# A decoder block's planned part: weight pages held through a seven-product pass, whole-tile additions on VectorE, longer transfer times in the planner

## The chip, the core and the metric

The kernel runs on one core of one Trainium2 chip. TensorE (PE) multiplies matrices into eight PSUM banks, VectorE (DVE), ScalarE (ACT) and GpSimd (POOL) do elementwise work, and SyncE (SP) issues most transfers between memory and the on-chip SBUF. The metric is the device time of one execution in microseconds; the median over several runs counts.

## The reference

One decoder layer for 1024 tokens of width 1024, all in float32:

```
h    = RMSNorm(x)
P    = h @ w_in                        # 1024 x 3584, split among the head groups
ret  = retention(rotary(rq), rotary(rk) / 8, rv)      # 8 heads of 64, chunks of 128, decaying state
ret  = RMSNorm per head(ret) * silu(rg)
dif  = (softmax(q1 k1) - lam * softmax(q2 k2)) v      # 4 heads, causal, RMS norm on q and k, per-head norm
x    = x + concat([ret, dif]) @ w_out
x    = x + (silu(h2 @ w_gate) * (h2 @ w_up)) @ w_down  # h2 = RMSNorm(x), inner width 2816
```

The columns rq, rk, rv, rg of `w_in` (512 each) belong to the retention heads; the change touches how their projection, the retention itself and the first feed-forward block are prepared.

## The kernel before

Each float32 product is made of three matmuls (`mm3`): a matrix is split into a high part `hi` (a cast, on ScalarE) and a low part `lo = a - hi` (a subtraction, on VectorE), and hi·hi, hi·lo and lo·hi are added up in a bank. So every weight tile of 128x512 needs a load, a cast and a subtraction before TensorE can use it (`halves_`).

The program has three parts. First the differential heads run, software-pipelined with their projection, to about 270 us. Last, from about 650 us, ten more blocks of the feed-forward part and the down projection run. Between them lies the **planned part**, which the change touches. It has no fixed loop order: each piece of work is a job with an engine, an estimated duration (`dur`, and `lag` for the time after a transfer's issue) and the pages it reads and writes. `Plan.times` runs a list scheduling over these estimates, in four rounds; each main job of TensorE gets a goal, and every other job a latest time counted back from the main jobs it serves (`AHEAD` us before) or from its `due`. The jobs are then issued in the order of planned times, and each engine keeps that order strictly: an instruction that waits holds up all behind it on its engine, and a transfer whose page is not free holds up all later ones on SP.

The planned part holds, in this order of TensorE's main work:

- Two **passes** (p = 0, 1, four heads each) over the retention projection, as a seven-product scheme for 2x2 blocks. Pass 0 has P4, P6, P7, P5, P3 left to do (P1 and P2 lie ahead), pass 1 has P1, P2, P6, P5, P3, P7, P4. Each product is 4 token tiles (j) of 4 contraction tiles (k), 12 matmuls per token tile. Its left operand is a block of `hT`, or a sum of blocks that was written to memory earlier and comes back through two pages (`x_sum`, transfers `raw<-sumd`). Its weights are blocks of `w_in` or signed sums of them, made in `prepare(p, name, k, n)`: load 256 KB blocks into pages (`rawload`, from the ring `wraw` of 13 pages named `spare`, `rowa`, `pr` in the profile), add, scale with the norm gain, split. Every product loads its own blocks anew. With a, b, d, c for the blocks (0,0), (0,1), (1,0), (1,1) of one k: P1 uses a, P2 d, P3 c, P5 a − b, P6 a − b + c, P7 b − c, P4 (d − c) − (a − b), up to the gains.
- Sixteen **retention units** (`unit(p, t)`): load a token tile's projections (`rowa<-cd`), rotary, transposes, two small score matmuls, decay mask, state update, output, per-head norm and gate. TensorE's parts of a unit (`m<-cs,wx` 128x128, `h<-wx,wy`, `h<-wy`, `h<-wy,wx`) stand between main matmuls.
- The **output projection** (`o_proj`, 16 products of 24 matmuls) with transposes of its input (`mix_turn`), then the second norm, transposes (`norm`) and block sums for the feed-forward part (`f_sum`).
- The **first feed-forward block**: seven products for w_gate and seven for w_up (`first_weights`, `first_product`), of whose weight sums five each add two tiles.

In the profile nearly all instructions have line 136, the helper that issues them; tile names tell them apart. `whi`/`wlo` are weight splits, `sx`, `act`, `sb`, `b`, `wo` hold operand blocks, `sum` and `raw` the sums, `wx` and `wy` the pages of the units, `h`, `pp`, `m` are banks.

Of the kernel before, what the change touches and what calls it, by code (L numbers as in the profile page):

```python
# [107 lines left out]
def block_kernel(ctx: ExitStack, tc: tile.TileContext, x, norm1_g, w_in, ret_norm_g, dq_g, dk_g,  # L108
# [685 lines left out]
    GAP, GAP_PE, AHEAD = 0.15, 0.6, 4.0  # L794
# [4 lines left out]
    def dma(to, src, r=(), w=(), **kw):  # L799
        return add("SP", 0.06, lambda: SY.dma_start(to, src), r, w, lag=2.6, **kw)  # L800
# [6 lines left out]
    def tt(to, a, b, op, r, w, eng="DVE", dur=0.78, **kw):  # L807
        e = V if eng == "DVE" else G
        return add(eng, dur, lambda: e.tensor_tensor(out=to, in0=a, in1=b, op=op), r, w, **kw)

    def stt(to, a, scalar, b, op0, op1, r, w, dur=0.78, **kw):
        return add("DVE", dur, lambda: V.scalar_tensor_tensor(out=to, in0=a, scalar=scalar, in1=b, op0=op0, op1=op1),
                   r, w, **kw)
# [24 lines left out]
    wraw = Ring([spare[i] for i in (0, 4, 5, 7, 1)] + rowk[4:8] + held)  # L838
# [7 lines left out]

    def rawload(p, kap, nu, k):
        key, page = wraw()
        dma(page.rearrange("p (a b) -> p a b", b=256), win_block(p, nu, 4 * kap + k), (), [key])
# [10 lines left out]
    def difference(p, k):  # L860
        (ka, a), (kb, b) = rawload(p, 0, 0, k), rawload(p, 0, 1, k)
        tt(a, a, b, ALU.subtract, [ka, kb], [ka], "POOL", 1.45)
        return (ka, a), (kb, b)

    def prepare(p, name, k, n):
        ga, gb = g1(k), g1(4 + k)
        if name in ("P1", "P2", "P3"):
            key, page = rawload(p, *{"P1": (0, 0), "P2": (1, 0), "P3": (1, 1)}[name], k)
            halves_(n, key, page, gb if name != "P1" else ga)
        elif name == "P5":  # L870
            (ka, a), _ = difference(p, k)
            halves_(n, ka, a, ga)
        elif name == "P6":
            (ka, a), (kb, b) = difference(p, k)
            kc, c = rawload(p, 1, 1, k)
            act_copy(b, a, [ka], [kb], ga)
            stt(c, c, gb, b, ALU.mult, ALU.add, [kb, kc], [kc])
            halves_(n, kc, c)
        elif name == "P7":
            (kb, b), (kc, c) = rawload(p, 0, 1, k), rawload(p, 1, 1, k)  # L880
            act_copy(c, c, [kc], [kc], gb)
            stt(b, b, ga, c, ALU.mult, ALU.subtract, [kb, kc], [kb])
# [3 lines left out]
        else:  # L886
            (ka, a), (kb, b) = difference(p, k)
            (kd, d), (kc, c) = rawload(p, 1, 0, k), rawload(p, 1, 1, k)
            tt(d, d, c, ALU.subtract, [kd, kc], [kd], "POOL", 1.45)
            act_copy(b, a, [ka], [kb], ga)  # L890
            stt(d, d, gb, b, ALU.mult, ALU.subtract, [kb, kd], [kd])
# [40 lines left out]
    for name in ("P4", "P6", "P7", "P5", "P3"):  # L932
# [4 lines left out]
        for j in range(4):  # L937
# [8 lines left out]
            elif name == "P7":  # L946
                tt(v, u, m, ALU.subtract, [bk, uk], [vk], dur=0.7)
                tt(d, d, v, ALU.subtract, [dk, vk], [dk], "POOL", 1.45)
# [64 lines left out]
    def unit(p, t, due=None):  # L1013
# [4 lines left out]
        for rk, r_, at in ((rck, rc, C_COS), (rnk, rn, C_SIN)):  # L1018
            tb = cs[:, at + t * 32:at + (t + 1) * 32].unsqueeze(1).broadcast_to([P, 16, 32])
            tt(r_.rearrange("p (g d) -> p g d", d=32), ca.rearrange("p (g d) -> p g d", d=32), tb, ALU.mult,  # L1020
               [cak], [rk], "DVE" if at == C_COS else "POOL", 0.78 if at == C_COS else 1.45)
# [3 lines left out]
        tt(q4[:, :, 0, :], rc4[:, :, 0, :], rn4[:, :, 1, :], ALU.subtract, [rck, rnk], [qk], "POOL", 0.8)  # L1025
        tt(q4[:, :, 1, :], rc4[:, :, 1, :], rn4[:, :, 0, :], ALU.add, [rck, rnk, qk], [qk], "POOL", 0.8)
        vk, vh = vh_r()
        tt(vh.rearrange("p (g d) -> p g d", d=HD), cb[:, 0:256].rearrange("p (g d) -> p g d", d=HD),
           vdec[:, t, 4 * p:4 * p + 4].unsqueeze(2).broadcast_to([P, 4, HD]), ALU.mult, [cbk], [vk], dur=0.46,
           )  # L1030
# [43 lines left out]
        def out_():  # L1074
# [15 lines left out]
        tt(onr[1].rearrange("p (g d) -> p g d", d=HD), o4, rs_.unsqueeze(2).broadcast_to([P, 4, HD]), ALU.mult,  # L1090
           ["b7o", sk], [onr[0]], dur=0.45)
        if p == 0 and t < 4:
            tt(gs, onr[1], gs, ALU.mult, [onr[0], gk_], [gk_], "POOL", 0.8)
# [462 lines left out]
```

## Time and profile before

| | |
|---|---|
| Median of 3 runs | 1241.63 us (1240.04 to 1241.9) |
| The profiled execution | 1242.88 us, of which the profile's span is 1240.8 us |
| TensorE, VectorE, ScalarE, GpSimd busy | 1196.0, 907.5, 570.6, 666.3 us |
| Mean granted TensorE clock | 0.99 |
| Planned part (from P4 to the end of the first feed-forward block) | 278.8 to 649.3 us |

A row of the groups gives engine, operation, output <- inputs, shape and count, then busy time and mean duration in ns of one, then the engine's idle time before them and what ended it. A row of the windows gives the stretch, its length, the busy time of each engine with its instruction count, the granted TensorE clock (1.00 is full speed), the busy share of the DMA engines and GB/s. A row of the transfers gives the queue, the count, the size and the median us from issue to landing. A row of a timeline gives start, duration, engine, operation, and in brackets the idle time before it and what ended it.

### The profile page before, as it was taken

The numbers are of one execution on the slowest core, as the hardware profiler recorded it, in microseconds if no ns is written. First come the engines' busy times: TensorE is split into PE (matmuls) and PEld (weight loads), VectorE is DVE, ScalarE is ACT, GpSimd is POOL, SyncE is SP. The second block draws the span as 40 slices with busy tenths as digits, with TensorE's granted clock in tenths as the row PEclk, the third lists the DMA queues.
The fourth block names the chain that finished last, engine by engine and source line by source line (L and its number), as shares of the span: only waits on it lengthen the run. The fifth ranks groups of instructions, "written<-read, shape, count | busy, mean of one in ns | idle before, by whom it ended". The sixth has DMA issues, their size and how long they took to land.

```text
span 1240.8 us, 17596 instructions
## 1 busy us (share of the span) xinstructions
PE 1196.0 (96%) x5872; PEld 1009.0 (81%) x5872; DVE 907.5 (73%) x1460; ACT 570.6 (46%) x1188; POOL 666.3 (54%) x728
## 2 busy tenths in 40 slices
PE   8999999999898999999979999999999999999998
PEld 7898989877677778887858888888888888888887
DVE  6988888866857975546898666666676659698697
ACT  6766555644434443334544434334334344444442
POOL 2678777562336746532576665455655447154053
PEclk9999999999999999999989999999999999999999
DMA  7166677269877753321223332233332268943332
GB/s 201 64 145 101 94 141 133 79 209 319 280 240 257 254 187 123 110 85 52 77 68 111 112 127 101 89 103 108 111 125 79 81 205 296 365 147 101 96 109 87
DMA packets 132953, 178.97 MB, mean 144 GB/s; under 512 B 12800, under 2 KB 77440, under 8 KB 132736
## 3 DMA queue, kind: packets, MB, share of 16 engines
q1 hardware_dynamic: 125920, 167.30, 41.5%
q0 software_dynamic: 5760, 10.49, 6.5%
q8 instruction: 46, 0.75, 0.3%
q14 instruction: 43, 0.35, 0.1%
q10 hardware_dynamic: 1184, 0.07, 0.1%
HBM read 125.65 MB, written 54.26 MB: 145 GB/s over the span
## 4 chain that ended last, share of the span: by engine, by line
PE 78%; DMA 6%; DVE 6%; POOL 4%; issue 3%; ACT 2%; SPq 0%; DVEq 0%; POOLq 0%; ACTq 0%
PE h L136 34%; PE pp L136 25%; PE m L136 17%; PE big L136 2%; DMA spare<-in_w_in_dram 2%; DVE wlo L136 1%; DMA raw<-sumd 1%; DMA rowa<-in_w_in_dram 1%; POOL sum L136 1%; POOL spare L136 1%; DVE pr L136 1%; POOL wx L136 0%; DMA sumd<-sumd 0%; ACT whi L136 0%; DVE sx L136 0%
## 5 line engine op out<-in xcount | busy, mean ns | idle before, releaser
L136 POOL TENSOR_TENSOR sum<-rawp 128x512 f32<-128x512 f32 x100 | 142.5, 1427 | 146.0 <-DVE wlo L136 141.3
L136 PE MATMUL pp<-whi,act 128*128 128x384 f32 (+1 forms) x624 | 191.7, 358 | 1.2 <-ACT whi L136 0.7
L136 ACT CAST whi<-sum 128x512 fp32r<-128x512 f32 x155 | 96.3, 622 | 198.6 <-PE h L136 65.1
L136 DVE TENSOR_TENSOR wlo<-sum,whi 128x512 fp32r<-128x512 f32 x155 | 154.2, 995 | 35.3 <-ACT whi L136 35.2
L136 POOL TENSOR_TENSOR sum<-wide 128x512 f32<-128x512 f32 x55 | 85.8, 1560 | 128.5 <-DVE wlo L136 98.9
L136 PEld LDWEIGHTS pp<-whi,act 128*128 128x128 f32 x624 | 116.2, 189 | 6.2 <-ACT whi L136 0.9
L136 PE MATMUL h<-sx,whi 128*128 128x512 f32 x360 | 112.6, 394 | 7.4 <-ACT rowa L136 7.1
L136 PE MATMUL pp<-wlo,act 128*128 128x384 f32 (+1 forms) x312 | 108.6, 348 | 0.6 <-DVE wlo L136 0.6
L136 DVE TENSOR_TENSOR wlo<-wide,whi 128x512 fp32r<-128x512 f32 x99 | 79.2, 824 | 32.9 <-ACT whi L136 32.8
L136 ACT CAST whi<-wide 128x512 fp32r<-128x512 f32 x99 | 59.4, 621 | 85.2 <-PE m L136 43.2
L136 PEld LDWEIGHTS h<-sx,whi 128*128 128x128 f32 x360 | 67.4, 189 | 21.6 <-ACT rowa L136 7.6
L136 POOL TENSOR_TENSOR fsum<-c 128x512 f32<-128x512 f32 x50 | 71.9, 1450 | 10.1 <-DMA ffd<-fsum 10.1
L136 PE MATMUL h<-whi 128*128 128x512 f32 x196 | 76.5, 390 | 0.0
L136 DVE TENSOR_TENSOR wlo<-rawp,whi 128x512 fp32r<-128x512 f32 x44 | 46.4, 1055 | 41.1 <-ACT whi L136 40.3
L136 DVE TENSOR_TENSOR c<-c,h 128x512 f32<-128x512 f32 x80 | 53.0, 683 | 32.1 <-PE h L136 32.0
L136 PE MATMUL h<-whi,wlo 128*128 128x512 f32 x196 | 76.3, 389 | 0.0
L136 PE MATMUL h<-wlo,whi 128*128 128x512 f32 x196 | 76.2, 389 | 0.0
L136 PE MATMUL h<-sx,wlo 128*128 128x512 f32 x180 | 70.5, 392 | 0.4 <-DVE wlo L136 0.4
L136 PEld LDWEIGHTS pp<-wlo,act 128*128 128x128 f32 x312 | 59.3, 190 | 3.6 <-DVE wlo L136 1.2
L136 PE MATMUL h<-b,whi 128*128 128x512 f32 x176 | 54.3, 390 | 0.0
L136 ACT ACTIVATE p<-big,nm 128x128 f32<-128x128 f32 (+7 forms) x64 | 47.7, 745 | 6.0 <-DVE nm L136 5.4
L136 DVE TENSOR_REDUCE nm<-big 128x1 f32<-128x128 f32 (+7 forms) x64 | 48.5, 758 | 2.2
(302 smaller groups left out, 3253.0 us busy)
## 6 DMA issues: line engine op xcount, KB each, us to landing
wide<-ffd SPq DMA_DIRECT2D x77, 256.0 KB, 2.8
spare<-in_w_in_dram SPq DMA_DIRECT2D x69, 256.0 KB, 4.7
ffd<-fsum SPq DMA_DIRECT2D x55, 256.0 KB, 2.0
rawp<-in_w_gate_dram SPq DMA_DIRECT2D x22, 512.0 KB, 3.7
rawp<-in_w_up_dram SPq DMA_DIRECT2D x22, 512.0 KB, 3.6
wide<-in_w_down_dram SPq DMA_DIRECT2D x44, 256.0 KB, 5.4
sumd<-act POOLq DMA_DIRECT2D x40, 256.0 KB, 5.6
rowa<-cd SPq DMA_DIRECT2D x32, 256.0 KB, 3.2
```

The costliest lines, as they stand in the source:

```text
L136: i = getattr(self.engine, op)(*(now(a) for a in args), **{k: now(a) for k, a in kw.items()})
```

## The change

- **Held weight pages.** In each pass P6 now loads a and c of each k into eight pages that stay for the pass (`keep_r`, `held_w`): a is overwritten with a − b, c stays. P5 and P3 split from these pages and load nothing, P7 loads only b, and pass 1's P4 only d. `wraw` has five pages left. P7 puts c times its gain into a page of its own.
- **From GpSimd to VectorE:** the weight differences, one subtraction of P7's outputs, in each unit the product with the sine, the two rotary halves and the gate product, the block sums 2, 5 and 6 and the weight sums of w_up.
- **From VectorE to ScalarE:** in each unit the scaling of v and of the output per head, each one operation of 256 columns, becomes four of 64 columns.
- **The planner's numbers:** a transfer occupies SP 0.8 us instead of 0.06, with 2.4 instead of 2.6 us behind it; VectorE operations count 0.74 or 0.75 instead of 0.78 or 0.8; `AHEAD` is 8 instead of 4 us; the units of tiles 4 to 7 are due at the projections of tiles 0 and 1.

```
-    GAP, GAP_PE, AHEAD = 0.15, 0.6, 4.0
+    GAP, GAP_PE, AHEAD = 0.15, 0.6, 8.0
-        return add("SP", 0.06, lambda: SY.dma_start(to, src), r, w, lag=2.6, **kw)
+        return add("SP", 0.8, lambda: SY.dma_start(to, src), r, w, lag=2.4, **kw)
-    def tt(to, a, b, op, r, w, eng="DVE", dur=0.78, **kw):
+    def tt(to, a, b, op, r, w, eng="DVE", dur=0.74, **kw):
-    def stt(to, a, scalar, b, op0, op1, r, w, dur=0.78, **kw):
+    def stt(to, a, scalar, b, op0, op1, r, w, dur=0.74, **kw):
...
-    wraw = Ring([spare[i] for i in (0, 4, 5, 7, 1)] + rowk[4:8] + held)
+    wraw = Ring(rowk[4:8] + [prk[8]])
+    keep_r = Ring([spare[i] for i in (0, 4, 5, 7, 1, 2, 6, 3)])
...
     g1 = lambda c: g1col[:, c:c + 1]
+    def load_raw(key, page, p, kap, nu, k):
+        dma(page.rearrange("p (a b) -> p a b", b=256), win_block(p, nu, 4 * kap + k), (), [key])
+
     def rawload(p, kap, nu, k):
         key, page = wraw()
-        dma(page.rearrange("p (a b) -> p a b", b=256), win_block(p, nu, 4 * kap + k), (), [key])
+        load_raw(key, page, p, kap, nu, k)
         return key, page
     def halves_(n, key, src, scale=None, reads=()):
...
         else:
             stt(lo, src, scale, hi.bitcast(F32), ALU.mult, ALU.subtract, [key, f"wh{n}"], [f"wl{n}"])
-    def difference(p, k):
-        (ka, a), (kb, b) = rawload(p, 0, 0, k), rawload(p, 0, 1, k)
-        tt(a, a, b, ALU.subtract, [ka, kb], [ka], "POOL", 1.45)
-        return (ka, a), (kb, b)
+    held_w = {}
     def prepare(p, name, k, n):
         ga, gb = g1(k), g1(4 + k)
-        if name in ("P1", "P2", "P3"):
-            key, page = rawload(p, *{"P1": (0, 0), "P2": (1, 0), "P3": (1, 1)}[name], k)
-            halves_(n, key, page, gb if name != "P1" else ga)
+        if name in ("P1", "P2"):
+            key, page = rawload(p, *{"P1": (0, 0), "P2": (1, 0)}[name], k)
+            halves_(n, key, page, ga if name == "P1" else gb)
+        elif name == "P6":
+            a, c = keep_r(), keep_r()
+            held_w[k] = a, c
+            (ka, a), (kc, c) = a, c
+            load_raw(ka, a, p, 0, 0, k)
+            kb, b = rawload(p, 0, 1, k)
+            load_raw(kc, c, p, 1, 1, k)
+            tt(a, a, b, ALU.subtract, [ka, kb], [ka])
+            act_copy(b, a, [ka], [kb], ga)
+            stt(b, c, gb, b, ALU.mult, ALU.add, [kb, kc], [kb])
+            halves_(n, kb, b)
         elif name == "P5":
-            (ka, a), _ = difference(p, k)
-            halves_(n, ka, a, ga)
-        elif name == "P6":
-            (ka, a), (kb, b) = difference(p, k)
-            kc, c = rawload(p, 1, 1, k)
-            act_copy(b, a, [ka], [kb], ga)
-            stt(c, c, gb, b, ALU.mult, ALU.add, [kb, kc], [kc])
-            halves_(n, kc, c)
+            halves_(n, *held_w[k][0], ga)
+        elif name == "P3":
+            halves_(n, *held_w[k][1], gb)
         elif name == "P7":
-            (kb, b), (kc, c) = rawload(p, 0, 1, k), rawload(p, 1, 1, k)
-            act_copy(c, c, [kc], [kc], gb)
-            stt(b, b, ga, c, ALU.mult, ALU.subtract, [kb, kc], [kb])
+            kb, b = rawload(p, 0, 1, k)
+            kt, t_ = wraw()
+            kc, c = held_w[k][1]
+            act_copy(t_, c, [kc], [kt], gb)
+            stt(b, b, ga, t_, ALU.mult, ALU.subtract, [kb, kt], [kb])
             halves_(n, kb, b)
         elif p == 0:
             halves_(n, *held[k])
         else:
-            (ka, a), (kb, b) = difference(p, k)
-            (kd, d), (kc, c) = rawload(p, 1, 0, k), rawload(p, 1, 1, k)
-            tt(d, d, c, ALU.subtract, [kd, kc], [kd], "POOL", 1.45)
-            act_copy(b, a, [ka], [kb], ga)
-            stt(d, d, gb, b, ALU.mult, ALU.subtract, [kb, kd], [kd])
+            (ka, a), (kc, c) = held_w[k]
+            kd, d = rawload(p, 1, 0, k)
+            tt(d, d, c, ALU.subtract, [kd, kc], [kd])
+            act_copy(a, a, [ka], [ka], ga)
+            stt(d, d, gb, a, ALU.mult, ALU.subtract, [ka, kd], [kd])
             halves_(n, kd, d)
     BLOCK = {"P1": hT[0][0], "P2": hT[0][1], "P4": hT[1][1], "P5": sxt[0], "P6": sbt, "P7": sxt[1], "P3": sxt[2]}
...
-                tt(d, d, v, ALU.subtract, [dk, vk], [dk], "POOL", 1.45)
+                tt(d, d, v, ALU.subtract, [dk, vk], [dk])
...
-               [cak], [rk], "DVE" if at == C_COS else "POOL", 0.78 if at == C_COS else 1.45)
+               [cak], [rk])
-        tt(q4[:, :, 0, :], rc4[:, :, 0, :], rn4[:, :, 1, :], ALU.subtract, [rck, rnk], [qk], "POOL", 0.8)
-        tt(q4[:, :, 1, :], rc4[:, :, 1, :], rn4[:, :, 0, :], ALU.add, [rck, rnk, qk], [qk], "POOL", 0.8)
+        tt(q4[:, :, 0, :], rc4[:, :, 0, :], rn4[:, :, 1, :], ALU.subtract, [rck, rnk], [qk], dur=0.46)
+        tt(q4[:, :, 1, :], rc4[:, :, 1, :], rn4[:, :, 0, :], ALU.add, [rck, rnk, qk], [qk], dur=0.46)
-        tt(vh.rearrange("p (g d) -> p g d", d=HD), cb[:, 0:256].rearrange("p (g d) -> p g d", d=HD),
-           vdec[:, t, 4 * p:4 * p + 4].unsqueeze(2).broadcast_to([P, 4, HD]), ALU.mult, [cbk], [vk], dur=0.46,
-           )
+
+        def scale_v():
+            for h in range(4):
+                A.activation(vh[:, h * HD:(h + 1) * HD], cb[:, h * HD:(h + 1) * HD], AF.Copy,
+                             scale=vdec[:, t, 4 * p + h:4 * p + h + 1])
+        add("ACT", 0.95, scale_v, [cbk], [vk])
...
-        tt(onr[1].rearrange("p (g d) -> p g d", d=HD), o4, rs_.unsqueeze(2).broadcast_to([P, 4, HD]), ALU.mult,
-           ["b7o", sk], [onr[0]], dur=0.45)
+
+        def scale_o():
+            for h in range(4):
+                A.activation(onr[1][:, h * HD:(h + 1) * HD], bank[7][:, h * HD:(h + 1) * HD], AF.Copy,
+                             scale=rs_[:, h:h + 1])
+        add("ACT", 0.95, scale_o, ["b7o", sk], [onr[0]])
-            tt(gs, onr[1], gs, ALU.mult, [onr[0], gk_], [gk_], "POOL", 0.8)
+            tt(gs, onr[1], gs, ALU.mult, [onr[0], gk_], [gk_], dur=0.46)
-            tt(m_[:, 256 * p:256 * p + 256], onr[1], gs, ALU.mult, [onr[0], gk_], [mk], "POOL", 0.8)
+            tt(m_[:, 256 * p:256 * p + 256], onr[1], gs, ALU.mult, [onr[0], gk_], [mk], dur=0.46, due=due)
...
+    DUE1 = {4: ("o", 0, 1), 5: ("o", 1, 1), 6: ("o", 1, 1), 7: ("o", 1, 1)}
+
-            unit(0, t)
-        unit(1, t)
+            unit(0, t, marks[DUE1[t]])
+        unit(1, t, marks[DUE1[t]] if t >= 4 else None)
...
-        eng, dur, e = ("POOL", 1.45, G) if b in (2, 5, 6) else ("DVE", 0.8, V)
+        eng, dur, e = ("DVE", 0.75, V)
...
-            eng, dur, e = ("POOL", 1.45, G) if o else ("DVE", 0.8, V)
+            eng, dur, e = ("DVE", 0.75, V)
```

Since the planner sets the order, the change moves instructions on all engines. Three places follow.

SP's queue where pass 0 begins: `mixdd<-rowa` spills rows of the differential heads' output (here those of the last two tiles), `in_w_in` are weight blocks, `raw<-sumd` the left operands' sums, `cd<-pr` results. Before:

```order
L136 DMA mixdd<-rowa 128x512
L136 DMA spare<-in_w_in_dram 128x2x256 x5
L136 DMA mixdd<-rowa 128x512
L136 DMA rowa<-in_w_in_dram 128x2x256 x2
L136 DMA spare<-in_w_in_dram 128x2x256
L136 DMA rowa<-in_w_in_dram 128x2x256
L136 DMA raw<-sumd 128x512 x2
```

Now:

```order
L136 DMA mixdd<-rowa 128x512
L136 DMA spare<-in_w_in_dram 128x2x256
L136 DMA mixdd<-rowa 128x512
L136 DMA spare<-in_w_in_dram 128x2x256
L136 DMA rowa<-in_w_in_dram 128x2x256
L136 DMA spare<-in_w_in_dram 128x2x256
L136 DMA rowa<-in_w_in_dram 128x2x256
L136 DMA spare<-in_w_in_dram 128x2x256
L136 DMA rowa<-in_w_in_dram 128x2x256
L136 DMA spare<-in_w_in_dram 128x2x256 x2
```

Four loads of P6 (of the first row's five; the other belongs to P4) moved from ahead of the last spill to behind it.

TensorE between the last matmuls of pass 1's P4 and the output projection: turns (`m<-cs,wx`), scores (`h<-wx,wy`), state (`h<-wy,wx`) and output (`h<-wy`) of units, and turns of the projection's input (`m<-cs,rowa`, `pp<-cs,pr`). Before:

```order
L136 MATMUL m<-cs,wx 128x128 x4
L136 MATMUL h<-wy 128x64 x4
L136 MATMUL h<-wy,wx 128x128 x2
L136 MATMUL m<-cs,rowa 128x128 x4
L136 MATMUL h<-wx,wy 128x256 x2
L136 MATMUL h<-wy,wx 128x128 x2
L136 MATMUL m<-cs,wx 128x128 x4
L136 MATMUL m<-cs,rowa 128x128 x4
```

Now:

```order
L136 MATMUL m<-cs,wx 128x128 x4
L136 MATMUL h<-wy,wx 128x128 x2
L136 MATMUL pp<-cs,pr 128x128 x4
L136 MATMUL m<-cs,rowa 128x128 x4
L136 MATMUL h<-wy,wx 128x128 x2
L136 MATMUL h<-wy 128x128
L136 MATMUL h<-wy 128x64 x2
L136 MATMUL h<-wy 128x128
L136 MATMUL h<-wy 128x64 x2
L136 MATMUL h<-wx,wy 128x256 x2
```

This run of small matmuls has 11 rows where it had 16 (both cut here); the units' remaining parts stand among the first seven products of the projection, where before they reached into the thirteenth.

VectorE at the end of the first feed-forward block: `rowa<-rowa,m` and `pr<-pr,pp` add products into outputs, `rowa<-rowa,pr` multiplies with the gate, `wlo<-sum,whi` and `wlo<-rawp,whi` are splits of the next block's weights. Before:

```order
L136 TENSOR_TENSOR wlo<-sum,whi 128x512
L136 TENSOR_TENSOR pr<-pr,pp 128x512
L136 TENSOR_TENSOR wlo<-sum,whi 128x512
L136 TENSOR_TENSOR rowa<-rowa,pp 128x512 x2
L136 TENSOR_TENSOR rowa<-rowa,m 128x512
L136 TENSOR_TENSOR wlo<-sum,whi 128x512
L136 TENSOR_TENSOR rowa<-rowa,m 128x512
L136 TENSOR_TENSOR rowa<-rowa,pr 128x512 x2
```

Now:

```order
L136 TENSOR_TENSOR rowa<-rowa,pp 128x512 x2
L136 TENSOR_TENSOR rowa<-rowa,h 128x512
L136 TENSOR_TENSOR pr<-pr,h 128x512
L136 TENSOR_TENSOR pr<-pr,pp 128x512
L136 TENSOR_TENSOR rowa<-rowa,m 128x512 x2
L136 TENSOR_TENSOR rowa<-rowa,pr 128x512 x4
L136 TENSOR_TENSOR wlo<-sum,whi 128x512
L136 TENSOR_TENSOR wlo<-rawp,whi 128x512
```

All splits of the next block moved behind the last addition and the four gate products. On TensorE the next block's first product stood among the last planned ones; now the first two matmuls of each of its first four products, eight in all, stand right behind the last planned one and their third waits for a split.

More of the change, by code (lines that the diff above doesn't have):

```diff
@@ L1242, in f_sum @@
         add("ACT", 0.62, lambda: A.copy(hi, opened["sum"][n]), [f"sum{n}"], [f"k{b}{p}h"], after=blk_after[b])
-        add("DVE", 0.8, lambda: V.tensor_tensor(out=lo, in0=opened["sum"][n], in1=hi.bitcast(F32), op=ALU.subtract),
+        add("DVE", 0.75, lambda: V.tensor_tensor(out=lo, in0=opened["sum"][n], in1=hi.bitcast(F32), op=ALU.subtract),
             [f"sum{n}", f"k{b}{p}h"], [f"k{b}{p}l"])
@@ L1291, in first_weights @@
         add("ACT", 0.65, lambda: A.copy(hi, src()), [key], [f"wh{at}"])
-        add("DVE", 0.8, lambda: V.tensor_tensor(out=lo, in0=src(), in1=hi.bitcast(F32), op=ALU.subtract),
+        add("DVE", 0.75, lambda: V.tensor_tensor(out=lo, in0=src(), in1=hi.bitcast(F32), op=ALU.subtract),
             [key, f"wh{at}"], [f"wl{at}"])
```

## The prediction

> **What bounds the kernel now.** I read the busy shares first, then the windows by stage, then what TensorE waited for, and last the chain and the groups where those waits are longest.
>
> ```profile
> PE 1196.0 (96%) x5872; PEld 1009.0 (81%) x5872; DVE 907.5 (73%) x1460; ACT 570.6 (46%) x1188; POOL 666.3 (54%) x728
> core 0: us, PE busy (x) PEld busy (x) DVE busy (x) ACT busy (x) POOL busy (x), PEclk, DMA share, GB/s
> 278.80:300.00 21.20, 18.96 (x72) 14.09 (x71) 12.96 (x18) 10.55 (x19) 6.72 (x5) 0.92 1.04 345
> 300.00:360.00 60.00, 53.46 (x230) 42.27 (x229) 43.10 (x58) 22.58 (x38) 16.87 (x12) 1.00 0.83 272
> 360.00:428.00 68.00, 60.77 (x285) 48.82 (x284) 52.39 (x74) 33.36 (x59) 44.35 (x43) 0.97 0.76 245
> 428.00:600.00 172.00, 166.24 (x894) 141.04 (x894) 108.57 (x184) 67.98 (x150) 77.27 (x108) 0.98 0.37 119
> 600.00:649.30 49.30, 40.53 (x189) 32.88 (x186) 44.52 (x52) 24.89 (x45) 35.40 (x22) 0.93 0.17 53
> 649.30:1200.00 550.70, 550.70 (x2430) 456.00 (x2431) 392.18 (x506) 224.92 (x387) 282.61 (x196) 1.00 0.42 137
> ```
>
> TensorE is the bound, and from 649.3 us on it never idles: 550.70 us for 2430 matmuls, 0.227 us each. The change touches only the planned part, 278.8 to 649.3. There TensorE idles 2.2, 6.5, 7.2, 5.8 and 8.8 us in the five stages, 30.5 together. To this comes a lowered clock: 0.92, 0.97, 0.98 and 0.93 of the stages' lengths leave 1.7, 2.0, 3.4 and 3.5 us, about 10.6. So some 41 us is all there is to win. The stages: the start of pass 0; the rest of pass 0 and the start of pass 1; the end of pass 1 with the retention units; the output projection; the first feed-forward block.
>
> **The loads of the passes.** From 278.8 to 428 the DMA engines are 76% busy or more. The second view has the weight loads of both passes, the third the chain at its longest wait.
>
> ```profile
> DMA packets 38095, 47.09 MB, mean 262 GB/s; under 512 B 2877, under 2 KB 27709, under 8 KB 38082
> spare<-in_w_in_dram SPq DMA_DIRECT2D x54, 256.0 KB, 5.0
> rowa<-in_w_in_dram SPq DMA_DIRECT2D x28, 256.0 KB, 5.0
> pr<-in_w_in_dram SPq DMA_DIRECT2D x6, 256.0 KB, 4.8
> 312.27 4.84 DMA raw<-sumd
> 317.14 0.63 ACT sx L136
> 317.79 0.70 DVE sx L136
> 318.51 2.85 DMA raw<-sumd
> raw<-sumd SPq DMA_DIRECT2D x10, 256.0 KB, 4.7
> raw<-in_x_dram SPq DMA_DIRECT2D x6, 256.0 KB, 2.9
> ```
>
> 54, 28 and 6 make 88 loads, as the code has it: 8 for each of four k in pass 0, 14 in pass 1. The change leaves 4 and 7, that is 44: 11.5 MB of the 47.1 MB of 270 to 450 us go, a quarter.
>
> What waits there is less the weights than the activation sums: sixteen tiles (`raw<-sumd`) pass through two pages. A page's round is load 4.84, split 0.63 and 0.70, 6.2 us together; TensorE eats two tiles in 24 matmuls, 5.45 us. Twelve of the tiles (P7, P5, P3) fall behind 300 us: six rounds, each 0.75 us too slow, make 4.5 of the 6.5 us idle in 300 to 360; I put the rest down to late weights. With a quarter less traffic the DMA share falls from 0.83 to about 0.62. The two landing rows bound the load: 4.7 us as in 300 to 333, 2.9 us as in 520 to 600, where the DMA engines have little else (119 GB/s and less). Between them in proportion to the share I take 4.0; the round is then 5.3 us, just under 5.45. **Gain 5 us**, the 4.5 and a little of the late weights; with 4.7 nothing, with 2.9 all 6.5.
>
> The Trainium skill ("DMA: Bandwidth & Descriptors", Anatomy of one DMA) puts a transfer at about 2.0 us plus its bytes at 436 GB/s, an estimate of 2.6 us for 256 KB. The trace disagrees: its median stays at 2.9 us where the engines are nearly free and at 4.7 us where they are busy. By the rule the gain here would be the whole 6.5 us.
>
> The start of pass 0 may lose. On SP's queue the last spill of the attention rows now stands ahead of all loads of P6; before, four of these were issued ahead of it.
>
> ```profile
> 269.25 5.88 SPq L136 DMA_DIRECT2D spare<-in_w_in_dram  x5
> 275.74 0.34 SPq L136 DMA_DIRECT2D mixdd<-rowa  x1
> ```
>
> Four loads of 0.26 MB at the 345 GB/s of this stage cost 3.0 us if they come last; in return half as many loads compete from 276 us on. The last weights of P6 pass a subtraction, two scalings and a split behind them. **0**, from a loss of 3.0 to a gain of 3.9 (idle and clock).
>
> **GpSimd's tiles on VectorE.** The rows are of 272 to 650 us.
>
> ```profile
> L136 POOL TENSOR_TENSOR sum<-pr 128x512 f32<-128x512 f32 x4 | 6.5, 1642 | 0.0
> L136 DVE TENSOR_TENSOR sx<-sum,sx 128x512 fp32r<-128x512 f32 x8 | 11.4, 1428 | 2.1 <-ACT sx L136 1.8
> L136 DVE TENSOR_TENSOR pr<-pr,h 128x512 f32<-128x512 f32 x26 | 17.6, 678 | 0.1
> L136 DVE TENSOR_TENSOR raw<-rawp 128x512 f32<-128x512 f32 x5 | 3.4, 690 | 0.1
> L136 DVE TENSOR_TENSOR wlo<-sum,whi 128x512 fp32r<-128x512 f32 x5 | 4.2, 849 | 2.5 <-ACT whi L136 2.5
> 599.53 0.68 DVE L136 TENSOR_TENSOR sum<-pr,rowa 128x512 f32<-128x512 f32 x1
> 600.13 0.69 DVE L136 TENSOR_TENSOR raw<-rawp 128x512 f32<-128x512 f32 x1
> 627.41 1.22 PE L136 MATMUL h<-sx,whi 128*128 128x512 f32 x2 [7.15 <-ACT rowa L136]
> 649.28 0.70 PE L136 MATMUL m<-b,whi 128*128 128x512 f32 x2 [0.66 <-DVE rowa L136]
> ```
>
> One addition of two tiles takes GpSimd 1.64 us and VectorE 0.69; back to back VectorE starts one each 0.60 us. And a VectorE operation with both inputs in SBUF takes 1.43 us beside GpSimd's additions, 0.69 where it has none beside it, while one that reads a PSUM bank keeps 0.68. So the two engines' additions run one after the other anyway, and what moves costs less than the wait it ends.
>
> *First feed-forward block.* 17 additions move (twelve block sums, five weight sums). VectorE has 52 operations in 44.5 us now; with 17 more, and the five splits `wlo<-sum` of the next block going later, it has 64: 38 us at 0.60, 44 at 0.68. TensorE has 40.5, less 3.5 of lost clock and less 2.7 for one product of the next block that stands in this stage only before. The stage without that product is 46.6 us now and would be about 41: 5.6 us. The 7.15 us wait should go: its releaser is ScalarE's copy of a bank into a `rowa` page, and GpSimd's late sums still read those pages.
>
> But the seam gets worse. Before, the next block's first splits stand between the last planned operations of VectorE, and the wait there is 0.66 us. Now they stand behind the last addition and four gate products: 0.68, four times 0.60 and 0.68 for the split make 3.8 us, against eight matmuls (1.8 us) that TensorE has ready. That is 2.0 us instead of 0.7. **Gain 4 us** net; bounds 0 (VectorE at 0.68 and the whole 3.8 exposed) and 12.3 (neither idle nor lost clock).
>
> *Retention units*, sixteen of them:
>
> ```profile
> L136 POOL TENSOR_TENSOR wx<-rowa,cs 128x512 f32<-128x512 f32 x16 | 23.5, 1467 | 0.5
> L136 POOL TENSOR_TENSOR wx<-wx 128x256 f32<-128x256 f32 x32 | 27.7, 885 | 14.9 <-PE h L136 10.1 <-DVE wx L136 4.6
> L136 DVE TENSOR_TENSOR wx<-h,small 128x256 f32<-128x256 f32 x16 | 6.7, 420 | 6.3 <-POOL small L136 6.1
> L136 ACT ACTIVATE whi<-spare,g1col 128x512 fp32r<-128x512 f32 x16 | 10.9, 715 | 4.1 <-issue 4.0
> L136 ACT ACTIVATE wy<-rowa,rs 128x256 f32<-128x256 f32 x16 | 8.1, 509 | 22.8 <-DMA mixrd<-wy 15.0 <-POOL pr L136 7.8
> ```
>
> The rotary steps go from 1.47 and twice 0.89 on GpSimd, 3.2 us, to 2.2 on VectorE (two at 0.69, two at 0.42). Each head scaling goes from one VectorE operation of 0.42 to four on ScalarE. No 64-column scaling is in the trace: 0.715 for 512 and 0.509 for 256 columns continue to 0.35, four are 1.4 us one by one; bounds 1.0 if they overlap by a quarter, 2.0 at the 0.509 row. One unit's path is thus shorter by 1.0 and longer by 1.0 per scaling at its end: about even. ScalarE gains 32 times 1.4, 45 us, on 159 us busy in 370: it has room.
>
> What shortens is the wait in 360 to 428: GpSimd, 44 us busy there, makes the weight differences between the rotary steps, and matmuls wait for either. Differences fall from 24 to 12 and leave GpSimd. Of 7.2 us idle and 2.0 us of clock I take **5 us**, from 0 (the units' own chain is what decides) to 9.
>
> In 428 to 600 the units of t=4 to 7 now end by the middle of the projection instead of three quarters through; the second half is left with transposes alone, the first half is denser on VectorE and ScalarE. Of 5.8 and 3.4 us I take **4 us**, from a loss of 4 (the denser half idles as the end of pass 1 does now, at 7.2 of 68 us) to 9.
>
> **The sum:** 5 + 0 + 4 + 5 + 4 = 18 us. The profiled execution took 1242.88 us (span 1240.8 and 2.1 around it), 1.25 above the median of 1241.63: 1242.88 − 18 − 1.25 = 1223.6, so **1224 us**.
>
> **Rivals.** *More goes than I take* (0.14): the planner's transfer and VectorE times now stand near the measured ones (0.8 plus 2.4 us against 2.9 to 4.7; 0.74 against 0.69), so few waits come unplanned; six us of idle and none of the lost clock stay: 1242 − 35 = 1207. Against it: the seam and the dense units are new waits.
>
> *The loads were hidden* (0.11): rounds stay at 6.2 us since bursts, not the mean, set the landing, and the 5 us of pass 0 stay out, as do those of 360 to 428: 1234. For it speaks the SP order, in which the sums still stand between weights.
>
> *No change* (0.06): as that, and the seam and the dense half take back the rest: 1241.
>
> *Slower* (0.11): the clock. The granted clock drops where small matmuls stand close together:
>
> ```profile
> 520.00:528.50 8.50, 7.64 (x35) 7.10 (x34) 5.66 (x10) 3.26 (x7) 6.50 (x9) 0.60 0.34 92
> 627.00:632.00 5.00, 4.59 (x13) 3.63 (x14) 4.75 (x5) 2.72 (x6) 5.00 (x4) 0.63 0.31 97
> ```
>
> At 520 us TensorE was busy 7.64 of 8.5 us and still had 0.60: this is a run of unit matmuls and transposes. Twelve units now stand in the end of pass 1 and the first half of the projection, a stretch about as long as the third stage, 68 us. All of it at 0.60 costs 45 us; from 0.40 of it on the 18 us are gone, and 0.5 of it gives 1242 − 18 + 23 = 1247. Against it: the longest run of small matmuls now is cut by projection matmuls.
>
> The Trainium skill ("TensorE: Matmul & The Clock Gate", What's actually happening) has the clock halve after about 3.4 us idle. By that this rival falls away; the trace disagrees at 520 us, where 0.86 us of 8.5 were idle.
>
> **Chances.** My case 0.58, with its own range 1214 to 1234. A measurement here tells 0.2%, 2.5 us: faster 0.58 + 0.14 + 0.11 = 0.83, same 0.06, slower 0.11. The range of 8 in 10 leaves half of the best case and the slower one outside: 1208 to 1240.
>
> **What would show it.** DMA share 300 to 360 near 0.6 and `raw<-sumd` landing in 4 us; GpSimd below 10 us busy in the first feed-forward block and `sx<-sum,sx` at 0.69; a wait of 2 to 3 us at the seam; the clock at 0.95 or more over the units. I am wrong if the five stages together idle more than 20 us, or if `raw<-sumd` still lands in 4.7.

## The result, and the profile after

The changed kernel takes 1209.3 us (median of 4 runs, 1206.9 to 1210.8), the kernel before 1241.0 on the same chip. The ratio is 0.9743, with a 95% interval of 0.9724 to 0.9762: 31.7 us less. The forecast was 1224, with a range from 1208 to 1240: the direction held, and the gain was 1.8 times the 18 us of the sum.

The page's busy line, and the windows of the changed kernel, cut where it reaches the work at which the five stages of the kernel before began and ended:

```profile
PE 1188.1 (98%) x5872; PEld 1003.9 (83%) x5872; DVE 909.9 (75%) x1525; ACT 601.2 (50%) x1316; POOL 536.7 (44%) x619
core 0: us, PE busy (x) PEld busy (x) DVE busy (x) ACT busy (x) POOL busy (x), PEclk, DMA share, GB/s
278.80:297.00 18.20, 17.85 (x79) 14.49 (x78) 14.17 (x22) 12.22 (x21) 0.00 (x0) 1.00 0.92 303
297.00:350.30 53.30, 52.80 (x223) 40.82 (x223) 44.54 (x70) 28.40 (x46) 1.00 (x2) 1.00 0.77 241
350.30:406.80 56.50, 56.50 (x278) 47.47 (x277) 46.19 (x81) 30.38 (x69) 6.81 (x11) 1.00 0.53 165
406.80:573.50 166.70, 163.30 (x888) 137.51 (x888) 113.39 (x206) 93.65 (x257) 37.47 (x62) 0.99 0.42 130
573.50:614.80 41.30, 38.58 (x191) 32.35 (x189) 40.20 (x67) 24.20 (x45) 3.16 (x3) 1.00 0.19 60
```

The five stages took 21.2, 60.0, 68.0, 172.0 and 49.3 us; they take 18.2, 53.3, 56.5, 166.7 and 41.3. That is 3.0, 6.7, 11.5, 5.3 and 8.0 us; of the last, about 2.7 us come back behind the seam, the border to the next block, so 5.3 are gained. These are four matmuls of the next block (0.9 us; before, twelve of them stood in this stage, now eight) and 1.9 us of a lowered clock that is shown below. Together 31.8 us, the difference of the two spans (1240.8 and 1209.0). The cuts follow the main products; a few of the units' small matmuls have moved across them, so the third and fourth figure may each be off by a us or two.

By cause it reads more simply. TensorE idled 30.5 us between 278.8 us and the seam, and idles 7.0 now. It is busy 329.0 us there instead of 340.0. Of these 10.9 us, 0.9 are the four matmuls; the other 10.0 are lowered clock that is gone, and 1.9 of them come back behind the seam. 23.5 and 10.0 less 1.9 make 31.6. The two largest of what TensorE still waits for from 270 to 650 us (3.0 us in four other rows):

```profile
PE h L136 <- DVE wlo L136: 2.3, 2, 2.0
PE h L136 <- DVE wy L136: 2.2, 2, 1.7
```

The columns are the total, the number of waits and the longest one. The longest is the seam that the prediction named, 1.98 us behind VectorE's four gate products, and the chain there shows how it ends:

```profile
611.01 0.75 DVE rowa L136 x2
...
612.22 1.89 DVE rowa L136 x3
614.11 0.61 DVE wlo L136
...
614.77 4.14 PE h L136 x10
618.91 2.29 PE m L136 x10
```

The ten matmuls behind the wait take 4.14 us, the ten after them 2.29: in this execution the wait costs almost as much again in clock. (The last section has other runs with the same wait where it does not.)

### The profile page after: what moved, and what is told of

It is laid out like the page before. It is cut to its first block, busy times and chain, and to the rows that moved or that the text cites. A ratio compares the mean times of both kernels' runs of the same rounds, so it can differ in the third digit from the quotient of the medians.

```text
span 1209.0 us, 17487 instructions
## 1 busy us (share of the span) xinstructions
PE 1188.1 (98%) x5872; PEld 1003.9 (83%) x5872; DVE 909.9 (75%) x1525; ACT 601.2 (50%) x1316; POOL 536.7 (44%) x619
## 4 chain that ended last, share of the span: by engine, by line
PE 82%; DVE 7%; DMA 5%; ACT 3%; issue 2%; POOL 2%; SPq 0%; ACTq 0%; DVEq 0%; POOLq 0%
PE h L136 37%; PE pp L136 25%; PE m L136 17%; PE big L136 2%; DMA raw<-sumd 2%; DVE wlo L136 1%; DMA spare<-in_w_in_dram 1%; DVE sx L136 1%; DVE sum L136 1%; ACT wx L136 0%; DVE wy L136 0%; DMA sumd<-sumd 0%; DMA more<-in_w_in_dram 0%; POOL spare L136 0%; DMA rowa<-in_w_in_dram 0%
## 5 line engine op out<-in xcount | busy, mean ns | idle before, releaser
L136 DVE TENSOR_TENSOR wlo<-sum,whi 128x512 fp32r<-128x512 f32 x155 | 158.0, 1019 | 34.0 <-ACT whi L136 33.6
```

What stands on the lines that cost most here:

```text
L136: i = getattr(self.engine, op)(*(now(a) for a in args), **{k: now(a) for k, a in kw.items()})
```

## The experiments

Each run was timed in five rounds beside the kernel before. "Above the changed kernel" is the difference of the two ratios to the kernel before, times 1240 us; both intervals together leave such a difference uncertain by about 3 us.

| run | what it is | ratio to before (95%) | us |
|---|---|---|---|
| `a_old_numbers` | after, all old planner numbers | 0.9804 (0.9790 to 0.9817) | 7.6 above after |
| `a_old_dma` | after, old transfer cost only | 0.9793 (0.9780 to 0.9807) | 6.2 above |
| `a_reload` | after, 88 weight loads (and 12 more differences on VectorE) | 0.9820 (0.9806 to 0.9833) | 9.5 above |
| `a_pool_ff` | after, 17 FF additions on GpSimd | 0.9841 (0.9828 to 0.9854) | 12.2 above |
| `a_port` | after, 17 idle additions on GpSimd | 0.9856 (0.9841 to 0.9870) | 14.0 above |
| `a_dve_scale` | after, head scalings on VectorE | 0.9849 (0.9836 to 0.9862) | 13.1 above |
| `a_pool_units` | after, rotary and gating on GpSimd | 0.9750 (0.9737 to 0.9763) | 0.9 above |
| `a_pool_diff` | after, weight differences on GpSimd | 0.9739 (0.9726 to 0.9752) | 0.5 below |
| `a_seam` | after, gate products behind three splits | 0.9722 (0.9708 to 0.9735) | 2.6 below |
| `b_new_numbers` | before, new planner numbers only | 0.9953 (0.9936 to 0.9970) | 5.8 below before |
| `b_held` | before, held weights only | 0.9934 (0.9923 to 0.9946) | 8.2 below before |
| `b_ff` | before, 17 FF additions on VectorE only | 0.9935 (0.9920 to 0.9949) | 8.1 below before |

### The loads of the passes: `a_reload` and `b_held`

`a_reload` puts before's rings and weight preparation back, with the differences on VectorE:

```
-    wraw = Ring(rowk[4:8] + [prk[8]])
-    keep_r = Ring([spare[i] for i in (0, 4, 5, 7, 1, 2, 6, 3)])
+    wraw = Ring([spare[i] for i in (0, 4, 5, 7, 1)] + rowk[4:8] + held)
...
+        elif name == "P5":
+            (ka, a), _ = difference(p, k)
```

where `difference` loads both of its weights again, as in the kernel before. So the run has not only 44 loads more: VectorE also makes 24 differences instead of 12 (1537 operations in all instead of 1525, 918.0 us busy instead of 909.9).

> The changed kernel with all 88 weight loads back (before's rings and weight preparation, differences on VectorE). Theory W: the 10 us that the stages from 278.8 to 336 us gained were the loads' doing; 1217 to 1220 us, raw<-sumd landing in 4.5 us or more. Rival (the traffic was hidden, the order did it): within 3 us of the changed kernel, 1209 to 1212 us.

It is 9.5 us above the changed kernel, but not where either theory had it. Windows of this run:

```profile
300.00:340.00 40.00, 39.11 (x170) 31.12 (x169) 36.13 (x58) 17.78 (x29) 0.00 (x0) 1.00 1.00 330
435.00:500.00 65.00, 56.80 (x325) 47.50 (x326) 50.98 (x99) 42.92 (x131) 19.90 (x28) 0.97 0.41 126
```

and of the changed kernel:

```profile
300.00:340.00 40.00, 39.50 (x164) 29.86 (x163) 33.85 (x54) 18.47 (x29) 0.00 (x0) 1.00 0.88 281
435.00:500.00 65.00, 62.67 (x360) 53.51 (x361) 50.55 (x99) 45.92 (x139) 21.59 (x33) 0.97 0.49 148
```

With the DMA engines busy all of 300 to 340 us, TensorE idles there 0.9 us instead of 0.5. The time goes later, 435 to 500 us: 8.2 us idle instead of 2.3, in a stretch of retention units. Which transfer, page or VectorE operation makes the late units later was not isolated. One candidate is their data (`rowa<-cd`, 340 to 440 us), in the changed kernel first and then in `a_reload`:

```profile
rowa<-cd SPq DMA_DIRECT2D x17, 256.0 KB, 2.8
```

```profile
rowa<-cd SPq DMA_DIRECT2D x19, 256.0 KB, 4.2
```

Against it: of the fifteen units whose first transposes the trace has, the first eleven start within 2.2 us of each other in the two runs; only the last four are 5.6 to 8.1 us late.

`b_held` does the opposite to the kernel before: the held pages alone, and the twelve differences that are left on GpSimd.

> The kernel before with held weights alone: 44 loads less, 12 of the 24 weight differences less, the rest still on GpSimd. By the prediction's first and third terms 5 to 10 us below before, ratio 0.992 to 0.996, with raw<-sumd landing in 4 us. Rival (transfers were not what the passes waited for): 0 to 3 us below, ratio 0.998 or more, and what goes comes from GpSimd's missing differences.

8.2 us below before, as the prediction's terms would have it; whether it is the loads or the twelve differences less on GpSimd, this run does not part; the activation sums land in 3.6 us here (300 to 333 us). The wait of the first feed-forward block stays (5.8 us, on the same `rowa` copy). So alone the held pages are worth about what undoing them costs.

### The planner's numbers: `a_old_numbers`, `a_old_dma` and `b_new_numbers`

```
-    GAP, GAP_PE, AHEAD = 0.15, 0.6, 8.0
+    GAP, GAP_PE, AHEAD = 0.15, 0.6, 4.0
-        return add("SP", 0.8, lambda: SY.dma_start(to, src), r, w, lag=2.4, **kw)
+        return add("SP", 0.06, lambda: SY.dma_start(to, src), r, w, lag=2.6, **kw)
-    def tt(to, a, b, op, r, w, eng="DVE", dur=0.74, **kw):
+    def tt(to, a, b, op, r, w, eng="DVE", dur=0.78, **kw):
```

(and 0.78 in `stt`). `a_old_dma` has the transfer line alone; `b_new_numbers` makes the same edits to the kernel before, the other way round.

> The changed kernel with the planner's old numbers alone (a transfer 0.06 us on SP plus 2.6, VectorE 0.78, AHEAD 4). Theory W (the work itself was the cost: fewer loads, shorter additions): the gain stays, 1209 to 1214 us. Theory P (the order was the cost: true transfer times place loads early enough): most of what the sum of the prediction missed comes from here, so 1218 us or more, with waits for weight splits back in 300 to 430 us.

> The changed kernel with the planner's old transfer cost alone (0.06 us on SP plus 2.6); AHEAD stays 8, VectorE 0.74. All old numbers together cost 7 to 8 us. If the transfer cost is what counts: 5 to 8 us above the changed kernel. Rival (the greater lead AHEAD covers late transfers by itself): within 2 us.

> The kernel before with the new planner numbers alone (a transfer 0.8 us on SP plus 2.4, VectorE 0.74, AHEAD 8). If the numbers are worth the same alone as in the changed kernel (undoing them there cost 7 to 8 us): 7 to 8 us below before, ratio 0.994. Rival (true times help only once the work has room, since GpSimd and the port still set the pace): within 2 us of before, ratio 0.998 to 1.002.

7.6 and 6.2 us above the changed kernel, 5.8 below the kernel before: the numbers are worth 6 to 8 us, in either kernel, and the transfer cost may be most of it (6.2 of 7.6, a difference within the uncertainty). No engine does other work for it, only the order changes. So neither theory has it alone: undoing the order costs about a fourth of the gain. Of the waits for weight splits that theory P expected one came back, of 1.9 us; the most, 3.7 us in three waits, is for ScalarE's work in the units. The prediction had no term for the numbers.

### The feed-forward block: `a_pool_ff`, `a_port` and `b_ff`

`a_pool_ff` puts the 17 additions back on GpSimd:

```
-        eng, dur, e = ("DVE", 0.75, V)
+        eng, dur, e = ("POOL", 1.45, G) if b in (2, 5, 6) else ("DVE", 0.75, V)
...
-            eng, dur, e = ("DVE", 0.75, V)
+            eng, dur, e = ("POOL", 1.45, G) if o else ("DVE", 0.75, V)
```

> The changed kernel with the additions of the first feed-forward block that were on GpSimd put back there (17). Theory W: the stage lost 5.3 us net through them, so 1214 to 1217 us, with a TensorE wait of 5 us or more near 590 us and sx<-sum,sx at 1.4 us. Rival (the wait there came from the late units in front, not from GpSimd): 1209 to 1211 us.

12.2 us above the changed kernel, more than twice the 5.3 that the stage gained. TensorE waits 7.8 us at one place in it. VectorE's groups there, 575 to 615 us, first in this run and then in the changed kernel:

```profile
L136 DVE TENSOR_TENSOR sx<-sum,sx 128x512 fp32r<-128x512 f32 x8 | 11.8, 1491 | 0.0
L136 DVE TENSOR_TENSOR wlo<-raw,whi 128x512 fp32r<-128x512 f32 x6 | 8.1, 1367 | 0.7 <-PE m L136 0.7
```

```profile
L136 DVE TENSOR_TENSOR sx<-sum,sx 128x512 fp32r<-128x512 f32 x8 | 5.2, 683 | 0.0
L136 DVE TENSOR_TENSOR wlo<-raw,whi 128x512 fp32r<-128x512 f32 x6 | 4.0, 686 | 0.0
```

The same splits take 1.4 to 1.5 us beside GpSimd's additions and 0.68 without them. Two causes are mixed here: a split that waits for a slow sum, and a VectorE that is held up. `a_port` parts them. It leaves every needed addition on VectorE and adds 17 that nobody needs:

```
+    def idle_add(made):
+        add("POOL", 1.45, lambda: G.tensor_tensor(out=TAB, in0=TAB, in1=TAB, op=ALU.subtract), (), ["tab"], after=[made])
```

once behind each moved sum in the plan. In the trace all 17 run in one row, from 568.4 to 592.6 us, so their times are not those of `a_pool_ff`. `TAB` is the cosine and sine table, which no unit reads any more at that point.

> The changed kernel plus 17 additions on GpSimd in the first feed-forward block that nobody waits for (a dead table minus itself). Theory C (GpSimd's additions cost since VectorE's operations with both inputs in SBUF last as long as the addition beside them): VectorE is busy all of this stage, so each costs it up to 1 us; 6 to 12 us above the changed kernel, most of what the same 17 cost when they were needed. Theory D (they cost since a split waits for their result): within 2 us.

14.0 us above the changed kernel, with nobody waiting for these additions. In the two traces the block itself is 11.9 us longer, from the same matmul ahead of it (564.70 and 562.43 us) to the end of the wait at the seam (614.77 and 624.43). So no wait for a sum is needed: that VectorE is held up is enough for all that `a_pool_ff` lost. The start of the block in this run, its windows and then single VectorE instructions (start, duration):

```profile
573.80:592.60 18.80, 15.26 (x69) 12.83 (x70) 18.77 (x16) 6.73 (x12) 17.78 (x13) 0.80 0.12 37
592.60:618.00 25.40, 23.31 (x95) 18.21 (x94) 25.33 (x43) 14.14 (x26) 2.15 (x2) 0.94 0.13 42
```

```profile
577.11 1.52 DVE L136 TENSOR_TENSOR act<-sum,act 128x512 fp32r<-128x512 f32 x1
578.56 1.52 DVE L136 TENSOR_TENSOR wlo<-rawp,whi 128x512 fp32r<-128x512 f32 x1
580.01 1.52 DVE L136 TENSOR_TENSOR act<-sum,act 128x512 fp32r<-128x512 f32 x1
581.45 0.68 DVE L136 TENSOR_TENSOR b<-pp,b 128x512 fp32r<-128x512 f32 x1
...
593.74 0.69 DVE L136 TENSOR_TENSOR raw<-rawp 128x512 f32<-128x512 f32 x1
594.34 1.29 DVE L136 TENSOR_TENSOR sx<-sum,sx 128x512 fp32r<-128x512 f32 x2
```

While the thirteen additions in this stretch run, one after the other, VectorE starts an operation each 1.45 us, in step with them; behind 592.6 us it starts one each 0.60. It gets 16 operations done in 18.8 us instead of about 30, and TensorE runs out of work (3.5 us idle, clock 0.80). Only the row that reads a PSUM bank (`pp`) keeps 0.68. The Trainium skill ("SBUF — State Buffer", Who interferes with whom) says that GpSimd and VectorE share a pair of ports under an exclusive lock, and that a VectorE instruction with two SBUF inputs contends with a GpSimd instruction that reads SBUF. The trace agrees, and adds the price: some 0.8 us of VectorE for each addition.

`b_ff` moves the same 17 in the kernel before, and nothing else.

> The kernel before with the 17 additions of the first feed-forward block on VectorE and nothing else. If the port is the cost there: as much as undoing it cost in the changed kernel, 9 to 13 us below before, ratio 0.990 to 0.993. By the prediction's term: 4 us below, 0.997. Rival (before, the block starts too late for other reasons and VectorE is the longer engine): within 2 us.

8.1 us below before. The 7.1 us wait is gone, the clock of the block is back from 0.93 to 1.00, and the seam of 2.0 us is there already:

```profile
600.00:650.00 50.00, 47.38 (x216) 39.14 (x216) 46.75 (x67) 24.63 (x45) 16.51 (x11) 1.00 0.23 75
```

### The other moves: `a_pool_units`, `a_pool_diff` and `a_dve_scale`

`a_pool_units` puts the sine product of each unit, the two steps behind it and the gating on GpSimd, of which one line of the rotary steps:

```
-        tt(q4[:, :, 0, :], rc4[:, :, 0, :], rn4[:, :, 1, :], ALU.subtract, [rck, rnk], [qk], dur=0.46)
+        tt(q4[:, :, 0, :], rc4[:, :, 0, :], rn4[:, :, 1, :], ALU.subtract, [rck, rnk], [qk], "POOL", 0.8)
```

`a_pool_diff` does so with the weight differences (eight of P6, four of P4) and the four tile differences of P7:

```
-            tt(a, a, b, ALU.subtract, [ka, kb], [ka])
+            tt(a, a, b, ALU.subtract, [ka, kb], [ka], "POOL", 1.45)
```

`a_dve_scale` has one operation on VectorE for four on ScalarE, twice in each unit, of which the second:

```
-        add("ACT", 0.95, scale_o, ["b7o", sk], [onr[0]])
+        tt(onr[1].rearrange("p (g d) -> p g d", d=HD), o4, rs_.unsqueeze(2).broadcast_to([P, 4, HD]), ALU.mult,
+           ["b7o", sk], [onr[0]], dur=0.45)
```

> The changed kernel with the rotary steps and the gating of the units back on GpSimd (weight differences stay on VectorE). Theory W by the prediction's third and fourth terms: 5 to 9 us of the gain are theirs, 1214 to 1218 us. Rival: GpSimd has room for them once the weight differences are off it, 1209 to 1212 us.

> The changed kernel with its weight differences (eight of P6, four of P4) and the four tile differences of P7 back on GpSimd. If the passes' waits were GpSimd's additions and what they do to VectorE beside them: 4 to 8 us above the changed kernel, with idle TensorE again in 278 to 430 us. Rival (16 additions of 1.6 us are hidden once half as many are needed): within 2 us.

> The changed kernel with the two head scalings of a unit back on VectorE (one operation instead of four on ScalarE). The prediction called this part even: within 2 us of the changed kernel. Rival: VectorE is 85% busy over the units, so 32 operations more on it cost 2 to 5 us.

The first two cost nothing: 0.9 us above, 0.5 below. GpSimd with the rotary steps on it is still only 64% busy from 360 to 500 us (89.9 of 140), and VectorE without them 67% (93.6): both have room for what the port costs. The third costs 13.1 us. Windows of 415 to 500 us, first the changed kernel, then `a_dve_scale`:

```profile
415.00:500.00 85.00, 81.63 (x473) 69.61 (x473) 66.94 (x132) 59.71 (x180) 26.31 (x40) 0.98 0.52 161
```

```profile
415.00:500.00 85.00, 76.01 (x411) 62.66 (x409) 68.04 (x140) 33.27 (x73) 23.71 (x31) 0.94 0.44 138
```

VectorE is as busy in both, 67 and 68 us; but with the scalings on it TensorE gets through 411 matmuls instead of 473, idles 9.0 us instead of 3.4, and loses clock. Its waits from 400 to 510 us in `a_dve_scale`:

```profile
PE h L136 <- DVE wx L136: 4.7, 3, 2.4
PE pp L136 <- DVE wlo L136: 1.6, 2, 1.1
```

Both releasers are VectorE's own: rotary results and weight splits, which are not what was moved. They come late since the scalings stand in VectorE's queue with them. ScalarE is busy 33 us of these 85 without them. In the changed kernel (groups of 360 to 500 us) one costs it 0.34 us, and a chain row has four back to back in 0.94, just below the prediction's bounds of 1.0 to 2.0:

```profile
L136 ACT ACTIVATE wy<-rowa,vdec 128x64 f32<-128x64 f32 x60 | 15.9, 341 | 0.2 <-PE h L136 0.2
```

```profile
449.64 0.94 ACT wx L136 x4
```

### The seam: `a_seam`

```
                 self.weights(n)
+                if n == 2 and defer is not None:
+                    defer()
```

`defer`, defined further down in the kernel, holds the first block's four gate products and the sums behind them.

> The changed kernel with the four gate products of the first feed-forward block and the sums behind them behind the next block's third weight split. The wait at the seam is VectorE's four gate products in front of the first split: 2.0 us idle, and the ten matmuls behind it take 4.1 us instead of 2.3. If that reading holds: 3 to 4 us below the changed kernel (ratio to before 0.971). Rival (ScalarE or GpSimd at the seam decides, or the split is only late by another wait): within 1 us.

The wait is gone, and the ten matmuls in front of which it stood take 2.27 us; the chain in this run:

```profile
610.04 0.68 PE h L136 x3
610.73 0.45 PE m L136 x2
611.18 0.23 PE h L136
611.40 0.45 PE pp L136 x2
611.86 2.27 PE h L136 x10
614.12 2.27 PE m L136 x10
```

So the reading holds: against the changed kernel's profiled execution, 2.0 us of wait and 1.9 of clock are taken out at that place. The whole is 2.6 us below the changed kernel, which the uncertainty of 3 us does not settle by itself. Its ratio to the kernel before is the lowest of all runs, at 1205.3 us.

## Why the prediction was right or wrong

**The bound and what there is to win: right.** 41 us of idle and clock in the five stages was the whole stake; 31.7 of it went, all of it there.

**Rest of pass 0, 5 us: right size, wrong mechanism.** The idle went from 6.5 to 0.5. But the step "between them in proportion to the share I take 4.0" failed: in the changed kernel the sums still land in 4.7 us, and the DMA share is 0.77, not 0.62:

```profile
raw<-sumd SPq DMA_DIRECT2D x9, 256.0 KB, 4.7
```

By the prediction's own sign I was wrong. What changed is the round itself. Counted over the twelve sums behind 297 us, two took 7.1 us before (first split at 300.66, last at 339.55), not the 6.2 of load and splits: some sums were also issued late after their page came free. The split of one page ends at 307.96 us in the rows of before below, and its next sum is issued at 310.12. In the changed kernel the longest such delay is 1.0 us. They take 6.3 now (297.66 to 332.17), and in `a_reload`, with all loads back, 5.9 (299.46 to 332.08).

```profile
300.66 0.61 ACT L136 CAST sx<-raw 128x512 fp32r<-128x512 f32 x1
...
307.27 0.69 DVE L136 TENSOR_TENSOR sx<-raw,sx 128x512 fp32r<-128x512 f32 x1 [1.46 <-ACT sx L136]
...
310.12 0.52 SPq L136 DMA_DIRECT2D raw<-sumd  x1
...
339.55 0.62 ACT L136 CAST sx<-raw 128x512 fp32r<-128x512 f32 x1 [2.42 <-DMA raw<-sumd]
```

```profile
297.66 0.60 ACT L136 CAST sx<-raw 128x512 fp32r<-128x512 f32 x1
...
332.17 0.62 ACT L136 CAST sx<-raw 128x512 fp32r<-128x512 f32 x1 [4.83 <-DMA raw<-sumd]
```

Not faster transfers but earlier issues shortened the round; and that is not one edit's doing, for `b_held`, with the old numbers, has two sums in 5.9 us too (298.95 to 331.17). The Trainium skill's sum for a transfer ("DMA: Bandwidth & Descriptors", Anatomy of one DMA), 2.6 us, fits neither kernel, with 4.7 us in both; the page gives that fit for transfers issued by GpSimd, and these go out on SP's queue.

**Start of pass 0, nothing: too small.** 3.0 us came of it, near the upper bound of 3.9; the late spill did no harm that can be seen.

**First feed-forward block, 4 us net: right mechanism, two terms mis-sized.** The wait went and the seam came, 1.98 us for the forecast 2.0. The stage gained 5.3. But the prediction took 2.7 us off the stage for a product of the next block and forgot that eight matmuls of that block would stand in it afterwards, though it counts them at the seam. Without the next block's matmuls and the wait at the seam, the stage took 45.9 us (49.3 less 2.7 and 0.7) and takes 37.5 (41.3 less 1.8 and 2.0): 8.4 us gained where the prediction had 5.6. Against them stand 1.3 us more wait at the seam, as forecast, and 1.9 us of lowered clock behind it, for which it had no term. That 5.3 came near 4 is partly luck. The moved additions are worth 8.1 us alone, and taken back they cost 12.2.

**360 to 428, 5 us: too small, and the reason stays open.** 9.2 us of idle and clock went. The prediction put it on GpSimd's rotary steps and weight differences, "matmuls wait for either"; putting either back alone costs nothing (both together were not put back). Nor does any run that undoes one part of the change bring the idle back: it is 1.3 us at most from 360 to 430 us, where before has 7.2. In the kernel before, the held pages alone bring it to 0.3:

```profile
360.00:428.00 68.00, 67.67 (x336) 56.53 (x334) 58.47 (x84) 29.92 (x54) 39.72 (x43) 1.00 0.58 188
```

So fewer loads, or twelve differences less on GpSimd, are enough there; from 430 to 510 us TensorE then idles 5.9 us instead of 1.7. In the changed kernel the parts stand in for one another, and which of them earned the gain is not shown.

**428 to 600, 4 us: right size, a term missing.** 5.3, of 9.2 in idle and clock. The prediction put it on the units that end earlier; no run takes back their due times alone. The step that failed lies in the units: the head scalings, which it called "about even", are worth 13.1 us, and it is here that they pay. In `a_dve_scale` TensorE is busy all of 360 to 415 us as in the changed kernel, and falls behind from 415 to 500. The working followed one unit's path, where four operations of 0.35 replace one of 0.42. The price lay in the queue: 32 operations fewer on the engine that the other units' steps and the splits wait for, 13.4 us at 0.42 each. So a single edit undone can cost more than its stage gained; that the others then leave no slack to hide it is a reading that no run tests.

**The planner's numbers** had no term at all, and are worth 6 to 8 us. The rival that gave them a price, "few waits come unplanned", named the end that came: 1207 for 1209.3. Its six us of idle are seven.

**Slower by the clock: refuted.** The dense stretch of units came, 473 matmuls in 85 us, and kept 0.98. The row at 627 us, read as a sign of small matmuls, stands behind the wait of 7.15 us. The one at 520 us counts 0.86 us idle, but another wait, of 1.12 us, ends just before it starts:

```profile
519.70 1.13 PE L136 MATMUL h<-wx,wy 128*128 128x256 f32 x4 [1.12 <-ACT wx L136]
```

So TensorE idled 1.98 us within 3.1 us there, and both rows of the prediction stand behind waits.

**The parts don't add up.** Undone one by one, the six parts cost 42.8 us, 11 more than there was to gain; the three that were made alone bring 22.1. One reading, which no run tests, is that each keeps the same few engines ahead of TensorE, and a loss at one is paid when the next is short too.

## What to carry to other kernels

Price a move by how full the two engines are around it, not by the path of one unit: the 32 operations taken off the fullest in-order engine were worth about their own time (13.1 us for 13.4), though on one unit's path the move looked even, and those put on an engine with room cost nothing. An addition on GpSimd beside a full VectorE costs VectorE the overlap even when nobody waits for its result; test it with idle additions. And a list scheduler's transfer times should lie near the measured ones: here 0.8 plus 2.4 us instead of 0.06 plus 2.6, where transfers land in 2.8 to 4.7, is worth 6 us without any work being changed.

## What the runs showed of the hardware that was not expected

One and the same wait of TensorE can cost clock or not. In the changed kernel the next 4 us behind the wait of 1.98 us run at little more than half the clock; with the wait gone, the same matmuls have 1.00. Windows in front of and behind the seam, then behind two other waits, changed kernel:

```profile
612.00:614.70 2.70, 0.79 (x4) 0.33 (x2) 2.70 (x6) 0.00 (x0) 0.51 (x1) 1.00 0.35 129
614.70:618.70 4.00, 3.93 (x10) 3.16 (x11) 4.00 (x4) 0.00 (x0) 4.00 (x3) 0.57 0.37 140
435.70:439.70 4.00, 3.96 (x21) 3.50 (x22) 3.73 (x6) 2.91 (x9) 1.20 (x2) 0.70 0.30 102
450.60:454.60 4.00, 3.95 (x26) 3.34 (x27) 2.47 (x7) 3.08 (x9) 0.61 (x1) 1.00 0.50 108
```

The third row stands behind a wait of 1.71 us, the fourth behind one of 0.81. But the wait of 1.98 us stands at the seam in nine of the traces. The ten matmuls behind it take 3.80 to 4.15 us in four (the changed kernel, `a_reload`, `a_old_dma`, `a_pool_diff`) and 2.56 to 2.60 in five (`a_old_numbers`, `a_port`, `a_pool_units`, `a_dve_scale`, `b_ff`), as in `a_pool_units`:

```profile
611.76 2.58 PE h L136 x10
```

In the kernel before, a wait of 2.46 us at 331.8 us is followed by 1.00 too. So a wait of 2 us may double its price, and no run shows what decides it. The Trainium skill ("TensorE: Matmul & The Clock Gate", What's actually happening) puts the fall at about 3.4 us idle; here less was enough, in four traces of nine.
